# A two-layer decoder trunk in fp32: inverse sums earlier, masks chained by head, the output weights fetched and split on another schedule

## The chip, the cores and the metric

The kernel runs on one core of one Trainium2 chip. The metric is the device time of one execution in microseconds (us). Five engines work side by side, each with its own list of instructions in a fixed order: TensorE (PE in the profile, with its weight loads as PEld), VectorE (DVE), ScalarE (ACT), GpSimd (POOL) and SyncE (SP). All DMAs of this stretch are issued by SP, one after the other in SP's order. An instruction starts when it is first in its engine's order and the semaphores it waits for have been raised.

## The reference, cut to what matters

Two layers work on x (1024 x 1024, fp32). Layer 0 mixes with causal pooling. Layer 1, where the change lies, mixes with a forgetting attention of 16 heads of 64 channels:

```python
logits = einsum('bqhd,bkhd->bhqk', q, k) * scale        # blocks of 128 queries
logits = logits + (cum_q[..., :, None] - cum_k[:, :, None, :])
logits = where(kpos <= qpos, logits, -inf)
p = softmax(logits)
out = einsum('bhqk,bkhd->bqhd', p, v)
...
h = x @ w_in                      # main | mem q | main gate | mem gate
y = concat([y_main * silu(g_main), y_mem * silu(g_mem)])   # 1024 + 512 channels
x = layer_norm(ALPHA * x + y @ w_out)                      # in each layer
```

Each layer also has a cross-attention of 4 heads to 256 memory tokens (y_mem).

## The kernel before, in words

**Tiling.** The sequence is 8 tiles of 128 rows, the channels 8 blocks of 128. A product in fp32 is made from three products of parts: every operand is split into a high part and the rest (`hi_lo`, L138: a copy on ACT at L140, a subtraction on DVE at L141). For weights that come in while the attention runs (`low[0]` set, L850) the split is on POOL (`gp_hi_lo`, L143: L144 and L145).

**Order.** PE's order is written out by hand: the attention and its fill run under a manual schedule of PE (L846 to L852). On ACT, DVE, POOL and SP a scheduler places the instructions, by their traced order and its own estimates, and adds the waits. So a line that stands earlier in the source need not stand earlier on its engine. The words of the changed kernel that pin or chain instructions bind this scheduler.

**Buffers.** Tiles are taken from pools by tag. Of the tag `raw` there are 4 buffers (L113). They hold the unsplit 128 x 512 pieces of all weights: those of a slab (`split_w`, L147 to L152, two pieces to a slab), those of W_out (`OutProj.fetch`, L345 to L351) and two pieces of y1d that `early` reads (L386). A new `raw` takes the buffer that was taken longest ago, and its DMA waits until that buffer's last reader is done. The split weights of slabs lie in the tag `w`, 6 buffers.

**A slab** (L169) is 48 matmuls of 512 columns: two weight pieces, two halves of the sequence, four blocks, three products. It yields after each, so that other code on PE can be put between them. `gate_units` (L259) is a slab whose two results go through `gate` (L190): tanh on ACT (L192), then one DVE instruction (L193).

**The attention** (`fox`, L781) goes over heads `hd` 0 to 16 and within a head over its eight tiles, from tile 7 (longest row of keys) down to tile 0; at `hd` 16 it only drains. One step of it is:

- `probs` (L692): one POOL instruction masks the diagonal block of the head's row tile R (L702). PE makes the logits in one or two parts (`mm3`, L167, into the two PSUM buffers of tag L). A DVE instruction for each part adds R and takes the running extreme (L709). Then comes `behind()`, which is `halves` of the step before (its inverse sum at L726 or L728 with the reciprocal of L729, then ACT L732 and DVE L733 for each part), and then the exponentials on ACT with their sums (L715).
- `fill.pump` (L52): so many matmuls of the waiting slabs.
- `turn` (L738): SP transposes the step-before probabilities by a DMA.
- `values` (L744): matmuls of probabilities and values for a pair of tiles, five steps behind, closed by ACT L758 and DVE L759. After an odd head `pair_out` (L764) multiplies with the gate on POOL and SP writes to y1d (L770).

R of the next head is asked for at the third step of a head (DMA from cumd).

**The last pair.** Heads 14 and 15 (`pr == 7`, L819) have 16 steps, `step` 0 to 15. Their fill is the slab of gate 7 (steps 0 to 3) and the late gates of pairs 3, 5 and 6 (`late_gate`, L772), one slab to four steps. A late gate reads its rows of y1d into an R buffer, multiplies on POOL (L778) and writes them back (L779). Beside this, W_out begins to come in: 24 pieces in all, of which `OutProj.fetch` issues the first ones and `split` splits them through `hi_lo`, and `early` (L382) reads and splits two pieces of y1d and later makes the first output products. In the kernel before, these calls stand ahead of `probs` in a step:

```python
if step == 7: lead = out_proj.early(...)
if step in (7, 9, 10, 12): next(lead)
out_proj.split(min(step - 1, 6) if step < 14 else step - 7)
out_proj.fetch(min(step + 1, 6) if step < 12 else min(step - 5, 8))
```

So piece 0 is fetched at step 0 and split at step 2, piece 5 is split at step 7, pieces 6 and 7 at steps 14 and 15. After the attention, `rest` (L394) splits the other 16 pieces and makes all the other output products (L376), and `norm` (L416) ends the layer.

Of the kernel before, what the change touches and what calls it, by code (L numbers as in the profile page):

```python
# [2 lines left out]

# [6 lines left out]
F32 = mybir.dt.float32  # L10
# [5 lines left out]
ALU = mybir.AluOpType  # L16
AX = mybir.AxisListType

P = 128
# [12 lines left out]
NEG = -1.0e30  # L32
# [39 lines left out]
def trunk_kernel(ctx, tc, x, xT, memT, win, wk, wv0, wv, wmk, wmv, wout, poolw, pscale, lng, lnb, bforget, out):  # L72
# [5 lines left out]
    nc = tc.nc  # L78
# [15 lines left out]
    def nm(tag):  # L94
        count[0] += 1
        return f"{tag}{count[0]}"

    def sb(shape, tag, bufs, dt=F32, where=None):
        return (where or pool).tile(shape, dt, tag=tag, name=nm(tag), bufs=bufs)

    def ps(shape, tag, bufs):
        return psum.tile(shape, F32, tag=tag, name=nm(tag), bufs=bufs)
# [7 lines left out]
    def MK(shape, dt=F32R):  # L110
        return sb(list(shape), "MK", 4, dt)

    def raw(shape):  # L113
        return sb(list(shape), "raw", 4)
# [4 lines left out]
    def tiny(n, dt=F32):  # L119
        return small.tile([P, n], dt, tag=f"s{n}{dt}", name=nm("s"), bufs=4 if n < 12 else 2)  # L120
# [14 lines left out]

        return tiles

    def hi_lo(hi, lo, src):  # L138

        nc.scalar.copy(hi, src)  # L140
        nc.vector.tensor_tensor(lo, src, hi.bitcast(F32), ALU.subtract)  # L141

    def gp_hi_lo(hi, lo, src):  # L143
        nc.gpsimd.tensor_scalar(hi, src, 1.0, 1.0, ALU.mult, ALU.mult)  # L144
# [19 lines left out]
    def mm3(acc, terms):  # L164

        for i, (a, b) in enumerate(terms):
            nc.tensor.matmul(acc, a, b, start=i == 0, stop=i == len(terms) - 1)  # L167
# [168 lines left out]
    class OutProj:  # L336
# [13 lines left out]
                nc.sync.dma_start(r, wout[self.l, n // 2 % 2, 2 * self.KKS[n // 4] + n % 2])  # L350
                self.raws.append(r)  # L351

        def split(self, upto):

            while self.n < upto:
                self.fetch(self.n + 1)
                n = self.n
                kk, nh, j = self.KKS[n // 4], n // 2 % 2, n % 2
                if j == 0:
                    self.ws[nh][kk] = self.wtile(n // 2)  # L360
                h, lo = self.ws[nh][kk]
                hi_lo(h[j], lo[j], self.raws.pop(0))
                self.n += 1

        def open(self, banks=(("pj", 3),) * 2 + (("L", 2),) * 2):
# [16 lines left out]
        def early(self, yh, yl):  # L382


            for j in range(2):
                r, two = raw([P, 2, 2 * P]), slice(2 * j, 2 * j + 2)  # L386
                nc.sync.dma_start(r, self.yd[2, :, two, : 2 * P])
                yield
                hi_lo(yh[:, two, :], yl[:, two, :], r)
                yield  # L390
            self.accs = self.open()
            yield from self.products(self.accs, 2, yh, yl)
# [79 lines left out]
    with tc.tile_pool(name="in0", bufs=1) as in0:  # L472
# [50 lines left out]
        out_proj = OutProj(0, w_slots(wtags, in0), y0d)  # L523
# [12 lines left out]
    with tc.tile_pool(name="in1", bufs=1) as in1:  # L536
# [135 lines left out]
        def start_units(own, following):  # L672
# [11 lines left out]
            next(gates)  # L684
            yield from islice(following, 30)

        def forget_rows(hd):
            R = sb([P, S], "R", 2, F32, in1)
            nc.sync.dma_start(R, cumd[hd].partition_broadcast(P))
            return R  # L690

        def probs(hd, i, R, sums, behind):  # L692

            q, kx, ky = pairs[hd // 2][hd % 2]
            L = (i + 1) * P
            qs = slice(i * P, L)  # L700
            p = MK([P, S], F32)
            nc.gpsimd.affine_select(R[:, qs], R[:, qs], [[-1, P]], ALU.is_ge, -NEG, base=0, channel_multiplier=1)  # L702
            m = tiny(2)
            top = -NEG
            parts = [(0, L)] if L <= NH else [(0, 384), (384, L)] if L == 640 else [(0, NH), (NH, L)]
            for n, (lo, up) in enumerate(parts):
                lg = ps([P, NH], "L", 2)[:, : up - lo]
                mm3(lg, ((q[:, qs], kx[:, lo:up]), (q[:, qs], ky[:, lo:up])))
                nc.vector.tensor_tensor_reduce(p[:, lo:up], lg, R[:, lo:up], 1.0, top, ALU.add, ALU.min, m[:, n : n + 1])  # L709
                top = m[:, n : n + 1]  # L710
            behind()
            es = []
            for n, (lo, up) in enumerate(parts):
                e = ps([P, NH], "T", 2)[:, : up - lo]
                nc.scalar.activation(  # L715
                    e, p[:, lo:up], AF.Exp, bias=top, scale=-1.0, accum_out=sums[:, n, hd % 2, i : i + 1],
                )
                es.append((lo, up, e))
            return hd, i, es, sums

        def halves(hd, i, es, sums):

            L, r = (i + 1) * P, tiny(1)
            one, two = (sums[:, n, hd % 2, i : i + 1] for n in range(2))
            if len(es) == 2:
                nc.vector.tensor_scalar(r, one, two, 1.0 / PSCALE, ALU.add, ALU.mult)  # L726
            else:
                nc.vector.tensor_scalar(r, one, 1.0 / PSCALE, None, ALU.mult)  # L728
            nc.vector.reciprocal(r, r)  # L729
            pair = sb([P, 2 * S], "P", 4, F16)  # L730
            for lo, up, e in es:
                nc.scalar.activation(pair[:, lo:up], e, AF.Copy, scale=r)  # L732
                nc.vector.scalar_tensor_tensor(pair[:, L + lo : L + up], e, r, pair[:, lo:up], ALU.mult, ALU.subtract)  # L733
            return hd, i, pair
# [46 lines left out]
        def fox(following, out_proj):  # L781
            fill, past, fresh = Fill(), [None] * LAG, [None]
            gs = {}

            def gate_ahead(pr):
                gs[pr] = G()
                fill.add(gate_units(win[1, 12 + pr], gs[pr], XH, XL), SLAB)

            ahead_R = forget_rows(0)
            for hd in range(HEADS + 1):  # L790
                pr, b = divmod(hd, 2)
                if hd == HEADS:
                    fill.add(lead, SLAB)
                if hd < HEADS:
                    if b == 0:
                        o, sums = G(), sb([P, 4 * ST], "sums", 2, F32, small).rearrange("p (n b i) -> p n b i", n=2, b=2)
                        if 0 < pr < 7:
                            fill.add(pair_units(pr + 1), 3 * SLAB)
                        for ahead in {0: (0, 1), 2: (2,), 4: (4,), 7: (7,)}.get(pr, ()):
                            gate_ahead(ahead)  # L800
                            if ahead == 0:
                                fill.add(following, SLAB)
                        for late in (3, 5, 6) if pr == 7 else ():
                            fill.add(late_gate(late), SLAB)
                    R, ahead_R = ahead_R, None
                for i in range(ST if hd < HEADS else LAG):
                    tile_of = ST - 1 - i
                    ahead = sum(SHARE[i:]) + (sum(SHARE) if b == 0 else 0)
                    part = fill.left * SHARE[i] / (ahead if hd < HEADS else sum(SHARE[i:LAG]))
                    new, split = None, []  # L810

                    def behind():
                        if fresh[0]:
                            split.append(halves(*fresh[0]))
                            fresh[0] = None

                    if i == 2 and hd < HEADS - 1:
                        ahead_R = forget_rows(hd + 1)
                    if pr == 7:  # L819
                        step = b * ST + i  # L820
                        if step == 7:
                            lead = out_proj.early(*(xy((P, 4, 2 * P)) for _ in range(2)))
                        if step in (7, 9, 10, 12):
                            next(lead)
                        out_proj.split(min(step - 1, 6) if step < 14 else step - 7)
                        out_proj.fetch(min(step + 1, 6) if step < 12 else min(step - 5, 8))
                    if hd < HEADS:
                        new = (hd, tile_of, o)
                        fresh[0] = probs(hd, tile_of, R, sums, behind)
                    else:  # L830
                        behind()
                    fill.pump(part * FRAC[0])
                    for what in split:
                        turn(*what)
                    older = past[0]
                    if older and older[1] % 2 == 0:
                        values(older[0], older[1] // 2, older[2])
                        if older[0] % 2:
                            pair_out(older[0] // 2, older[1] // 2, older[2], gs.get(older[0] // 2))
                    fill.pump(part * (1 - FRAC[0]))  # L840
                    past = past[1:] + [new]
                if b or hd == HEADS:
                    fill.pump(float("inf"))

        wtags = [("MK", 4), ("V", 4)] + [("B", 10)] * 4 + [("w", 0), ("MK", 4), ("R", 2), ("V", 4), ("PG", 0), ("B", 10)]
        out_proj = OutProj(1, w_slots(wtags, in1), y1d)  # L846
# [68 lines left out]
```

## Time and profile before

| What | us |
|---|---|
| Three runs | 1277.45, 1277.76, 1273.79; median 1277.45 |
| The profiled execution | 1275.16 |
| Its span | 1273.4 |
| PE busy within the span | 1243.5 |
| DVE busy | 803.8 |
| ACT busy | 578.5 |
| POOL busy | 174.2 |

The profile is of one execution, and its times are counted from the start of its span. The attention runs from about 672 to 1127 us, its last pair of heads from about 1057 us. A row of the timeline has start, duration, engine, line, operation, names of output and inputs, shape and a count of like instructions; in brackets stands how long the engine was idle before it and what released it. Starts and durations of matmuls overlap, since they are pipelined. L167 writing to L is a logits matmul, L167 writing to O a matmul of values, L179 a matmul of a slab. In the rows a stage by stage view gives (windows), the busy time and count of PE, PEld, DVE, ACT and POOL stand in this order, then the granted PE clock (1.00 is full) and the share and rate of the DMAs.

### The profile page before, as it was taken

The page shows a single profiled execution, that of the slowest core. Times are in us where ns is not written, and L with a number is a line of the kernel's source. Part 1 is how long each engine was busy: PE and PEld are TensorE (multiplying, and loading weights), DVE is VectorE, ACT ScalarE, POOL GpSimd, SP SyncE. Part 2 cuts the span into 40 slices and gives each one's busy share as a digit, 9 for nine tenths or more (in the row PEclk, how much of TensorE's full clock was granted, in tenths as well). Part 3 has the DMA queues.
Part 4 walks back from the last instruction along what each step waited for, and adds up shares of the span by engine and source line. Part 5 has one row for each costly group of instructions (what it writes and reads, how often), then busy time and mean ns, then how long its engine had stood idle before and what let it go on. Part 6 is the DMA issues. An engine that isn't in the chain of part 4 may idle for free. (4 is left out here: it accounts for less than half of the span.)

```text
span 1273.4 us, 19681 instructions
## 1 busy us (share of the span) xinstructions
PE 1243.5 (98%) x7018; PEld 1032.7 (81%) x7018; DVE 803.8 (63%) x1901; ACT 578.5 (45%) x1273; POOL 174.2 (14%) x276
## 2 busy tenths in 40 slices
PE   9999999999999999999999999999999999899997
PEld 6888888888888888888887778887887777777885
DVE  6444766376455555377456878777877887664644
ACT  5233643242321123266225777666667677652110
POOL 0000000000000000000013334342333323430000
PEclk9999999999999999999999999999999999999999
DMA  6333444232553324244516786867877687884430
GB/s 224 108 100 100 117 117 132 83 119 89 158 197 100 106 84 134 75 116 115 162 51 180 137 184 155 195 157 175 187 160 178 157 196 171 209 224 149 166 115 34
DMA packets 267427, 178.66 MB, mean 140 GB/s; under 512 B 212288, under 2 KB 225728, under 8 KB 267328
## 3 DMA queue, kind: packets, MB, share of 16 engines
q1 hardware_dynamic: 267328, 177.40, 52.3%
q8 instruction: 55, 0.90, 0.3%
q14 instruction: 44, 0.36, 0.1%
HBM read 94.97 MB, written 22.61 MB: 92 GB/s over the span
## 5 line engine op out<-in xcount | busy, mean ns | idle before, releaser
L179 PE MATMUL pj<-A,w 128*128 128x512 f32 x2928 | 723.4, 395 | 0.8 <-ACT A L140 0.8
L179 PEld LDWEIGHTS pj<-A,w 128*128 128x128 f32 x2928 | 536.5, 188 | 103.9 <-ACT A L140 2.4
L141 DVE TENSOR_TENSOR w<-raw,w 128x512 fp32r<-128x512 f32 x106 | 74.0, 700 | 105.9 <-ACT w L140 105.1
L715 ACT ACTIVATE T<-MK,s 128x512 f32<-128x512 f32 x192 | 110.8, 577 | 53.1 <-DVE s L709 39.6
L140 ACT CAST w<-raw 128x512 fp32r<-128x512 f32 x106 | 65.7, 621 | 149.8 <-PE pj L179 103.0
L733 DVE SCALAR_TENSOR_TENSOR P<-T,s,P 128x512 f16<-128x512 f32 x192 | 111.5, 613 | 29.8 <-ACT P L732 27.6
L732 ACT ACTIVATE P<-T,s 128x512 f16<-128x512 f32 x192 | 102.7, 576 | 45.5 <-issue 17.2
L167 PE MATMUL L<-B,B 128*128 128x512 f32 (+3 forms) x384 | 92.0, 344 | 14.5 <-DVE s L709 14.1
L167 PEld LDWEIGHTS L<-B,B 128*128 128x128 f32 x384 | 69.8, 188 | 36.8 <-DVE s L709 23.9
L619 POOL MEMSET G<- 128x128 f32 x1 | 0.2, 205 | 610.2 <-DVE V L333 610.2
L709 DVE CUSTOM_DVE_ANT_0 MK<-L,R 128x512 f32<-128x512 f32 (+3 forms) x128 | 72.9, 570 | 12.0 <-PE L L167 7.2
L167 PEld LDWEIGHTS <-V 128*128 128x128 f16 x1152 | 65.2, 99 | 18.6 <-issue 18.6
L167 PE MATMUL O<-T,V 128*128 128x128 f16 x1152 | 76.2, 221 | 1.1 <-DVE G L759 1.1
L141 DVE TENSOR_TENSOR T<-T,T 128x1024 fp32r<-128x1024 f32 x23 | 28.1, 1223 | 70.2 <-PE L L376 51.3
L145 POOL TENSOR_TENSOR w<-raw,w 128x512 fp32r<-128x512 f32 x54 | 70.6, 1307 | 3.8
L140 ACT CAST T<-T 128x1024 fp32r<-128x1024 f32 x23 | 24.2, 1050 | 98.4 <-DMA T<-y0d 50.6
L702 POOL TENSOR_SCALAR_AFFINE_SELECT R<-R 128x128 f32<-128x128 f32 x128 | 42.7, 336 | 180.4 <-DVE s L709 99.2
L144 POOL TENSOR_SCALAR w<-raw 128x512 fp32r<-128x512 f32 x54 | 35.8, 664 | 139.9 <-PE pj L179 131.3
L212 PE MATMUL pj<-T,w 128*128 128x256 f32 x384 | 48.7, 284 | 0.9 <-DVE w L141 0.8
L212 PEld LDWEIGHTS pj<-T,w 128*128 128x128 f32 x384 | 47.6, 192 | 2.0 <-DVE w L141 1.3
L376 PE MATMUL pj<-B,T 128*128 128x512 f32 x186 | 46.5, 392 | 0.5 <-DVE T L141 0.5
L376 PE MATMUL L<-B,T 128*128 128x512 f32 x174 | 43.0, 391 | 0.0
(214 smaller groups left out, 1598.1 us busy)
## 6 DMA issues: line engine op xcount, KB each, us to landing
raw<-in_win_dram SPq DMA_DIRECT2D x96, 256.0 KB, 2.8
raw<-in_wout_dram SPq DMA_DIRECT2D x48, 256.0 KB, 2.9
B<-B SPq DMA_DIRECT2D x32, 256.0 KB, 4.0
R<-cumd SPq DMA_DIRECT2D x16, 512.0 KB, 4.3
y0d<-Y SPq DMA_DIRECT2D x12, 512.0 KB, 3.1
T<-y0d SPq DMA_DIRECT2D x12, 512.0 KB, 3.9
T<-y1d SPq DMA_DIRECT2D x11, 512.0 KB, 4.3
raw<-in_wmk_dram SPq DMA_DIRECT2D x16, 256.0 KB, 2.6
```

The source lines that it names most:

```text
L140: nc.scalar.copy(hi, src)
L141: nc.vector.tensor_tensor(lo, src, hi.bitcast(F32), ALU.subtract)
L145: nc.gpsimd.tensor_tensor(lo, src, hi.bitcast(F32), ALU.subtract)
L167: nc.tensor.matmul(acc, a, b, start=i == 0, stop=i == len(terms) - 1)
L179: nc.tensor.matmul(accs[n], a[:, k, :], b[:, kt, n * NH : (n + 1) * NH], start=kt == 0 and i == 0, stop=kt == KT - 1 and i == 2,)
L212: nc.tensor.matmul(acc, w[:, k, :], m[pc][:, k, :], start=pc == 0 and k == 0 and i == 0, stop=pc == 1 and k == 3 and i == 2,)
L376: nc.tensor.matmul(accs[a][nh], y[:, k, a * P : (a + 1) * P], w, start=kt == 8 and i == 0, stop=kt == 7 and i == 2,)
L702: nc.gpsimd.affine_select(R[:, qs], R[:, qs], [[-1, P]], ALU.is_ge, -NEG, base=0, channel_multiplier=1)
L709: nc.vector.tensor_tensor_reduce(p[:, lo:up], lg, R[:, lo:up], 1.0, top, ALU.add, ALU.min, m[:, n : n + 1])
L715: nc.scalar.activation(e, p[:, lo:up], AF.Exp, bias=top, scale=-1.0, accum_out=sums[:, n, hd % 2, i : i + 1],)
L732: nc.scalar.activation(pair[:, lo:up], e, AF.Copy, scale=r)
L733: nc.vector.scalar_tensor_tensor(pair[:, L + lo : L + up], e, r, pair[:, lo:up], ALU.mult, ALU.subtract)
```

## The change

It has four parts. (1) `inverse_of` is taken out of `halves` and is called inside `probs` of the next tile, behind the first part's DVE instruction. (2) Each mask on POOL is bound to come behind the mask traced before it, so that the masks stand in order of heads and steps. (3) In the last pair the fetches of W_out follow a new list by step, ahead of `probs`; the splits follow another list, behind `probs`, and are pinned: an instruction handed to `keep_in_program_order` stays behind all that was traced before it on its engine. The pieces are split one to a step from step 3 to step 8 (before: steps 2 to 7), the last two at steps 13 and 14. `early` begins at step 9, with its two reads at steps 9 and 12 ahead of `probs` and its two splits at steps 11 and 15 behind it (before: 7, 9, 10, 12). (4) The two splits of `early` are pinned as well. No arithmetic, shape or count of instructions changes.

```diff
--- before.py
+++ after.py
@@ -1,4 +1,4 @@
-from contextlib import ExitStack
+from contextlib import ExitStack, nullcontext
 from itertools import islice
 
 import concourse.bass as bass
@@ -135,10 +135,11 @@
 
         return tiles
 
-    def hi_lo(hi, lo, src):
-
-        nc.scalar.copy(hi, src)
-        nc.vector.tensor_tensor(lo, src, hi.bitcast(F32), ALU.subtract)
+    def hi_lo(hi, lo, src, pinned=False):
+
+        pin = tc.keep_in_program_order if pinned else lambda ins: ins
+        pin(nc.scalar.copy(hi, src))
+        pin(nc.vector.tensor_tensor(lo, src, hi.bitcast(F32), ALU.subtract))
 
     def gp_hi_lo(hi, lo, src):
         nc.gpsimd.tensor_scalar(hi, src, 1.0, 1.0, ALU.mult, ALU.mult)
@@ -350,7 +351,7 @@
                 nc.sync.dma_start(r, wout[self.l, n // 2 % 2, 2 * self.KKS[n // 4] + n % 2])
                 self.raws.append(r)
 
-        def split(self, upto):
+        def split(self, upto, pinned=False):
 
             while self.n < upto:
                 self.fetch(self.n + 1)
@@ -359,7 +360,7 @@
                 if j == 0:
                     self.ws[nh][kk] = self.wtile(n // 2)
                 h, lo = self.ws[nh][kk]
-                hi_lo(h[j], lo[j], self.raws.pop(0))
+                hi_lo(h[j], lo[j], self.raws.pop(0), pinned)
                 self.n += 1
 
         def open(self, banks=(("pj", 3),) * 2 + (("L", 2),) * 2):
@@ -386,7 +387,7 @@
                 r, two = raw([P, 2, 2 * P]), slice(2 * j, 2 * j + 2)
                 nc.sync.dma_start(r, self.yd[2, :, two, : 2 * P])
                 yield
-                hi_lo(yh[:, two, :], yl[:, two, :], r)
+                hi_lo(yh[:, two, :], yl[:, two, :], r, True)
                 yield
             self.accs = self.open()
             yield from self.products(self.accs, 2, yh, yl)
@@ -684,12 +685,14 @@
             next(gates)
             yield from islice(following, 30)
 
+        masked = []
+
         def forget_rows(hd):
             R = sb([P, S], "R", 2, F32, in1)
             nc.sync.dma_start(R, cumd[hd].partition_broadcast(P))
             return R
 
-        def probs(hd, i, R, sums, behind):
+        def probs(hd, i, R, sums, inverse, behind):
 
 
 
@@ -699,7 +702,10 @@
             L = (i + 1) * P
             qs = slice(i * P, L)
             p = MK([P, S], F32)
-            nc.gpsimd.affine_select(R[:, qs], R[:, qs], [[-1, P]], ALU.is_ge, -NEG, base=0, channel_multiplier=1)
+            with tc.issue_after(masked[-1]) if masked else nullcontext():
+                masked.append(
+                    nc.gpsimd.affine_select(R[:, qs], R[:, qs], [[-1, P]], ALU.is_ge, -NEG, base=0, channel_multiplier=1).ins
+                )
             m = tiny(2)
             top = -NEG
             parts = [(0, L)] if L <= NH else [(0, 384), (384, L)] if L == 640 else [(0, NH), (NH, L)]
@@ -708,6 +714,8 @@
                 mm3(lg, ((q[:, qs], kx[:, lo:up]), (q[:, qs], ky[:, lo:up])))
                 nc.vector.tensor_tensor_reduce(p[:, lo:up], lg, R[:, lo:up], 1.0, top, ALU.add, ALU.min, m[:, n : n + 1])
                 top = m[:, n : n + 1]
+                if n == 0:
+                    inverse()
             behind()
             es = []
             for n, (lo, up) in enumerate(parts):
@@ -718,15 +726,19 @@
                 es.append((lo, up, e))
             return hd, i, es, sums
 
-        def halves(hd, i, es, sums):
-
-            L, r = (i + 1) * P, tiny(1)
+        def inverse_of(hd, i, n, sums):
+            r = tiny(1)
             one, two = (sums[:, n, hd % 2, i : i + 1] for n in range(2))
-            if len(es) == 2:
+            if n == 2:
                 nc.vector.tensor_scalar(r, one, two, 1.0 / PSCALE, ALU.add, ALU.mult)
             else:
                 nc.vector.tensor_scalar(r, one, 1.0 / PSCALE, None, ALU.mult)
             nc.vector.reciprocal(r, r)
+            return r
+
+        def halves(hd, i, es, r):
+
+            L = (i + 1) * P
             pair = sb([P, 2 * S], "P", 4, F16)
             for lo, up, e in es:
                 nc.scalar.activation(pair[:, lo:up], e, AF.Copy, scale=r)
@@ -809,6 +821,11 @@
                     part = fill.left * SHARE[i] / (ahead if hd < HEADS else sum(SHARE[i:LAG]))
                     new, split = None, []
 
+                    def inverse():
+                        if fresh[0]:
+                            old, k, es, of = fresh[0]
+                            fresh[0] = old, k, es, inverse_of(old, k, len(es), of)
+
                     def behind():
                         if fresh[0]:
                             split.append(halves(*fresh[0]))
@@ -818,17 +835,21 @@
                         ahead_R = forget_rows(hd + 1)
                     if pr == 7:
                         step = b * ST + i
-                        if step == 7:
+                        out_proj.fetch((0, 1, 2, 3, 4, 5, 6, 6, 6, 6, 7, 7, 8, 8, 8, 8)[step])
+                        if step == 9:
                             lead = out_proj.early(*(xy((P, 4, 2 * P)) for _ in range(2)))
-                        if step in (7, 9, 10, 12):
+                        if step in (9, 12):
                             next(lead)
-                        out_proj.split(min(step - 1, 6) if step < 14 else step - 7)
-                        out_proj.fetch(min(step + 1, 6) if step < 12 else min(step - 5, 8))
                     if hd < HEADS:
                         new = (hd, tile_of, o)
-                        fresh[0] = probs(hd, tile_of, R, sums, behind)
+                        fresh[0] = probs(hd, tile_of, R, sums, inverse, behind)
                     else:
+                        inverse()
                         behind()
+                    if pr == 7:
+                        out_proj.split((0, 0, 0, 1, 2, 3, 4, 5, 6, 6, 6, 6, 6, 7, 8, 8)[step], True)
+                        if step in (11, 15):
+                            next(lead)
                     fill.pump(part * FRAC[0])
                     for what in split:
                         turn(*what)
```

## The prediction, made before the changed kernel had run

> **What bounds the kernel now.** The first part of the page gives the busy time of each engine; the view of waits, kept to PE, gives what PE waited for.
>
> ```profile
> PE 1243.5 (98%) x7018; PEld 1032.7 (81%) x7018; DVE 803.8 (63%) x1901; ACT 578.5 (45%) x1273; POOL 174.2 (14%) x276
> ```
>
> ```profile
> PE L L167 <- DVE s L709: 14.1, 15, 3.1
> ```
>
> PE is busy for 1243.5 of 1273.4 us, and its list of instructions is the same in both kernels, row for row. So time can come only from PE's pauses and its clock. Nearly half of the pauses are one kind: 15 waits of the logits matmuls (L167) for a DVE extreme (L709) that has yet to empty their buffer, 14.1 us in all. The change is about these. I then looked for the 15 in PE's timeline; the largest lie in the last pair.
>
> ```profile
> 1070.74 2.91 PE L179 MATMUL pj<-A,w 128*128 128x512 f32 x12
> 1076.03 0.73 PE L167 MATMUL L<-B,B 128*128 128x512 f32 x2 [2.39 <-DVE s L709]
> 1076.60 1.32 PE L179 MATMUL pj<-A,w 128*128 128x512 f32 x5
> ...
> 1102.82 0.73 PE L167 MATMUL L<-B,B 128*128 128x512 f32 x2 [3.11 <-DVE s L709]
> 1104.01 0.50 PE L167 MATMUL L<-B,B 128*128 128x256 f32 x2 [0.46 <-DVE s L709]
> ```
>
> What held DVE stands in the timelines of ACT and DVE:
>
> ```profile
> 1070.48 0.62 ACT L140 CAST B<-raw 128x512 fp32r<-128x512 f32 x1 [1.90 <-DMA raw<-in_wout_dram]
> ...
> 1098.41 1.32 ACT L140 CAST B<-raw 128x512 fp32r<-128x512 f32 x2 [3.87 <-DMA raw<-in_wout_dram]
> ```
>
> ```profile
> 1071.63 0.49 DVE L759 SCALAR_TENSOR_TENSOR G<-O,unscale,G 64x256 f32<-64x256 f32 x1 [1.17 <-ACT G L758]
> ...
> 1072.23 0.68 DVE L141 TENSOR_TENSOR V<-raw,V 128x512 fp32r<-128x512 f32 x1
> ...
> 1074.83 0.68 DVE L193 SCALAR_TENSOR_TENSOR G<-G,pj 128x512 f32<-128x512 f32 x1
> 1075.42 0.55 DVE L709 CUSTOM_DVE_ANT_0 MK<-L,R 128x384 f32<-128x384 f32 x1
> ...
> 1101.18 0.21 DVE L726 TENSOR_SCALAR s<-sums 128x1 f32<-128x1 f32 x1 [4.88 <-ACT T L715]
> ...
> 1102.08 0.67 DVE L709 CUSTOM_DVE_ANT_0 MK<-L,R 128x512 f32<-128x512 f32 x1
> ```
>
> Both times a copy of a W_out piece stands on ACT ahead of the work that DVE needs, and ACT waits for that piece's DMA: 1.90 and 3.87 us. DVE then waits behind ACT (for L758 at 1071.63, for the exponentials at 1101.18), and L709 comes late, at 1075.42 and 1102.08. After the second pause the clock falls as well, as three windows of 3.41 us show:
>
> ```profile
> 1098.17:1101.58 3.41, 1.54 (x7) 0.94 (x5) 0.36 (x2) 3.07 (x7) 2.77 (x5) 1.00 0.45 114
> 1101.58:1104.99 3.41, 1.71 (x7) 1.18 (x8) 2.96 (x8) 2.33 (x6) 0.89 (x2) 1.00 0.57 191
> 1104.99:1108.40 3.41, 3.41 (x19) 2.64 (x19) 2.65 (x9) 2.26 (x6) 1.57 (x2) 0.50 0.97 211
> ```
>
> PE was granted 0.50 for one window, so about 1.7 us of work was lost there. After the pause of 2.39 us nothing of this kind follows (PE's five matmuls at 1076.60 take 1.32 us, the rate of the twelve at 1070.74).
>
> **What the change removes.** In the last pair the copies and subtractions of W_out now stand behind the exponentials of their step, and each piece has been on its way two steps or more. The three pauses, 2.39 + 3.11 + 0.46, and the 1.7 of clock go: 7.66 us. What is late next is named below. At worst the clock loss stays, for other reasons: 5.96.
>
> Elsewhere the order of the masks matters:
>
> ```profile
> 759.02 0.54 POOL L702 TENSOR_SCALAR_AFFINE_SELECT R<-R 128x128 f32<-128x128 f32 x2 [6.66 <-DMA R<-cumd]
> ```
>
> ```profile
> 759.60 0.48 DVE L709 CUSTOM_DVE_ANT_0 MK<-L,R,s 128x256 f32<-128x256 f32 x1 [0.80 <-POOL R L702]
> ```
>
> ```profile
> 764.59 0.73 PE L167 MATMUL L<-B,B 128*128 128x512 f32 x2 [1.08 <-DVE s L709]
> ...
> 878.54 0.72 PE L167 MATMUL L<-B,B 128*128 128x512 f32 x2 [1.12 <-DVE s L709]
> ...
> 992.31 0.74 PE L167 MATMUL L<-B,B 128*128 128x512 f32 x2 [0.95 <-DVE s L709]
> ...
> 1045.28 0.73 PE L167 MATMUL L<-B,B 128*128 128x512 f32 x2 [1.21 <-DVE s L709]
> ```
>
> POOL waits 6.66 us for the R of the *next* head while a mask of the current head stands behind it; DVE loses 0.80 us by that and PE stalls five us later. The same pattern stands ahead of the pauses at 878.54 and 992.31. Together they are 3.15 us. In order of heads the masks don't wait so, but DVE is also crowded there by other work, so I take two thirds, 2.2 (0 to 3.15). The moved inverse is two one-column instructions; they sit in front of or behind an L709 of the same step. In the built order nothing else of DVE or ACT moves up to about 1028 us, so there I count the move at nothing: it is hidden by DVE's idle time. Ahead of the pause at 1045.28 one DVE instruction of 0.7 us (L657) goes from in front of the L709 to behind it: 0.7 of the 1.21 (0 to 1.21). Gains outside the last pair: 2.9 us (0 to 4.36).
>
> **What the change adds.** W_out pieces and slab weights share four `raw` buffers. A later split holds a buffer longer, and in the built order of the changed kernel the DMA of late gate 3's first weight piece waits for the DVE subtraction of W_out piece 0. That subtraction is pinned at step 3. The scheduler has put on DVE, in front of it, the closing instruction of gate 7 (L193), and on ACT, in front of its copy, the tanh of gate 7 and the two exponentials of step 3. So it can't run until gate 7's *last* matmul is done. But after that matmul PE has only the two logits matmuls of the next tile, and then late gate 3's first matmul, which needs the piece. The wait is a chain from the end of one slab to the start of the next. Its links, from the groups by shape between 640 and 1130 us, and from two issues with their POOL split:
>
> ```profile
> L192 ACT ACTIVATE G<-pj 128x512 f32<-128x512 f32 x16 | 9.5, 592 | 6.7 <-PE pj L179 5.4 <-PE L L167 1.3
> ...
> L715 ACT ACTIVATE T<-MK,s 128x384 f32<-128x384 f32 x48 | 27.5, 574 | 2.7 <-DVE P L733 2.4
> L715 ACT ACTIVATE T<-MK,s 128x256 f32<-128x256 f32 x48 | 22.3, 465 | 4.9 <-DVE s L709 3.6 <-DVE P L733 1.3
> ...
> L140 ACT CAST B<-raw 128x512 fp32r<-128x512 f32 x10 | 6.1, 620 | 7.9 <-DMA raw<-in_wout_dram 5.8 <-DMA raw<-y1d 2.0
> ...
> L144 POOL TENSOR_SCALAR w<-raw 128x512 fp32r<-128x512 f32 x54 | 35.8, 664 | 139.9 <-PE pj L179 131.3 <-DMA raw<-in_win_dram 8.5
> L145 POOL TENSOR_TENSOR w<-raw,w 128x512 fp32r<-128x512 f32 x54 | 70.6, 1307 | 3.8
> ```
>
> ```profile
> 1068.34 0.38 SPq L149 DMA_DIRECT2D raw<-in_win_dram  x1
> ...
> 1074.75 0.33 SPq L149 DMA_DIRECT2D raw<-in_win_dram  x1
> ```
>
> ```profile
> 1071.71 0.63 POOL L144 TENSOR_SCALAR w<-raw 128x512 fp32r<-128x512 f32 x1 [5.77 <-DMA raw<-in_win_dram]
> ...
> 1077.45 0.62 POOL L144 TENSOR_SCALAR w<-raw 128x512 fp32r<-128x512 f32 x1 [2.73 <-DMA raw<-in_win_dram]
> ```
>
> *First wait.* Tanh 0.59, exponentials 0.57 + 0.47, copy 0.62, subtraction 0.68: 2.93 us. From SP's issue to POOL's start 3.37 (1068.34 to 1071.71) or 2.70 (1074.75 to 1077.45). POOL's high part 0.66. Together 6.29 to 6.96 behind gate 7's end; PE is ready 0.57 behind it (1076.03 to 1076.60), so it waits 5.7 to 6.4. The third matmul needs the low part, 1.31 later, of which two matmuls cover 0.5: 0.8 more. 6.5 to 7.2; I take 6.9. In the kernel before, the issue at 1068.34 lies 5 us ahead of gate 7's end, since its buffer came free earlier; hence no such pause there.
>
> *Second wait.* The second piece of late gate 3 waits for the subtraction of W_out piece 2, at step 5, behind the exponential of tile 2. From that tile's logits: L709 0.55, exponential 0.57, copy 0.62, subtraction 0.68, with small steps 2.5; then 2.70 to 3.37 and 0.66: 5.9 to 6.5.
>
> ```profile
> 1080.14 2.92 PE L179 MATMUL pj<-A,w 128*128 128x512 f32 x12
> 1082.91 0.40 PE L167 MATMUL L<-B,B 128*128 128x256 f32 x2
> 1083.14 1.09 PE L179 MATMUL pj<-A,w 128*128 128x512 f32 x4
> ```
>
> PE's work up to the matmul that needs it is the like of these rows, 1080.14 to 1083.14: 3.0. It waits 2.9 to 3.5, with the low part's 0.8 3.7 to 4.3; I take 4.0.
>
> *Third wait.* The first piece of late gate 6 waits for the subtraction of `early`'s first piece (step 11), which again stands behind the end of a slab, late gate 5; on SP it stands also behind a write of y1d that waits for two POOL products.
>
> ```profile
> 1097.89 2.81 POOL L778 TENSOR_TENSOR R<-R,G 128x256 f32<-128x256 f32 x4 [4.92 <-DMA R<-y1d]
> ```
>
> Logits 0.57, L709 0.67 and its read, L193 0.68, two products 1.4: 3.4; issue to POOL 2.70 to 3.37, high part 0.66: 6.8 to 7.4, less 0.57, plus 0.8: 7.0 to 7.7; I take 7.4. For the other pieces (late gate 5's two, late gate 6's second) the same counting gives no pause.
>
> The three are 18.3 us (17.2 to 19.2). Each has a bare pause as long as the 3.11 us that cost a window at 0.50, or longer: 3 x 1.7 = 5.1 us of clock. Bounds: 1.7, if one alone is caught, and 8.5, if each of the two long ones costs two windows.
>
> [...]
>
> Behind the last pair the order of `rest` shifts a little. Its largest pause is this:
>
> ```profile
> 1140.35 0.50 PE L167 MATMUL O<-T,V 128*128 128x128 f16 x6 [1.11 <-DVE G L759]
> ```
>
> It may go or be doubled: 0, with bounds of -1.1 and +1.1.
>
> **The sum,** against the profiled execution's own 1275.16 us (2.3 below the median of the runs): - 7.66 - 2.9 + 18.3 + 5.1 = **1288 us**. Low end: 1275.16 - 7.66 - 4.36 + 17.2 + 1.7 - 1.1 = 1280.9. High end: 1275.16 - 5.96 + 19.2 + 8.5 + 1.1 = 1298.
>
> **The rivals.** *The shared buffers don't hold PE* (ends on the other side). If the pieces of the late gates land ahead of the slab's end, as the one issued at 1068.34 did, only the gains are left: 1275.16 - 7.66 - 2.9 = 1264.6. It decides by whether the subtraction of W_out piece 0 runs some 6 us ahead of gate 7's end. For it: ACT and DVE are busy for only 45% and 63% of the span. Against it: the built order puts the tanh of gate 7's end in front, and an engine doesn't pass over what stands first.
> *Only one of the three waits reaches PE,* because after the first pause the other engines are ahead: 1264.6 + 6.9 + 1.7 = 1273 to 1275.
> *Longer landings.* One W_out issue took from 1093.94 to ACT's 1098.41:
>
> ```profile
> 1093.94 0.86 SPq L350 DMA_DIRECT2D raw<-in_wout_dram  x2
> ```
>
> That is 4.47 us, 1.4 more than my middle value of 3.04; three times this, and the clock's upper bound, give 1288 + 4.2 + 3.4 = 1295.6.
> *No clock loss:* 1288 - 5.1 = 1283.
> *Masks and inverse do nothing outside the last pair,* since the pauses come from a crowded DVE and not from the mask: 1288 + 2.9 = 1291.
>
> **Chances.** Forecast as summed 0.45, longer landings 0.15, masks without effect 0.12, no clock loss 0.10, one wait alone 0.06, no wait 0.07, worse than all of this 0.05. The range 1280 to 1299 holds the first four, 0.82. What a measurement of this kernel can tell from no change is about 0.3%, 3.8 us, so 1273.6 to 1281.3 counts as the same: faster 0.07, same 0.06, slower 0.87.
>
> **What would show it.** In the changed kernel's profile PE should show three pauses released by POOL (w, L144 or L145) in front of L179: of some 6, 3 and 6 to 7 us, at the starts of late gate 3, its second piece and late gate 6, each with a pause of about 0.8 behind it, and windows at 0.50 behind them. The pauses named L709 in the last pair should be gone, ACT's waits for raw<-in_wout_dram too, and the pauses near 764, 878 and 992 smaller. POOL's waits for R<-cumd should shrink from the 6.66 us shown. I am wrong if POOL's L144 doesn't wait for raw<-in_win_dram behind the slabs' ends.

## The result, and the profile after

| | us | runs |
|---|---|---|
| Before, median | 1276.39 (1273.79 to 1277.76) | 5 |
| Changed, median | 1289.53 (1287.31 to 1290.61) | 5 |
| Ratio | 1.0102, 95% interval 1.0087 to 1.0117 | |
| Span of the profiled execution, before and changed | 1273.4 and 1288.6 | |

The changed kernel is slower by 13.1 us in the medians and by 15.2 us in the profiled spans. The forecast was 1288. In the changed source the lines stand a little lower: L709 is L715 now, L144 and L145 are L145 and L146, L167 is L168, L179 is L180, L702 is L707, L759 is L771. These are PE's line of the page, and PE's waits of 2 us and more:

```profile
PE 1248.5 (97%) x7018; PEld 1036.2 (80%) x7018; DVE 803.2 (62%) x1901; ACT 578.9 (45%) x1273; POOL 172.0 (13%) x276
```

```profile
PE pj L180 <- POOL w L145: 18.7, 3, 8.1
PE L L168 <- DVE s L715: 4.5, 10, 0.9
PE O L168 <- DVE G L771: 2.3, 1, 2.3
```

A wait that was not there, on POOL's split of slab weights, came three times and holds 18.7 us. The wait that the change is about fell from 14.1 to 4.5. PE is busy for 5.0 us longer with the same matmuls, which the windows further down put down to the clock. And a wait for values (L771) grew from 1.1 to 2.3. Together: + 18.7 - 9.6 + 5.0 + 1.2 = + 15.3, against 15.2 of span. Nothing else of size is left to explain.

The three pauses in PE's timeline, with the logits ahead of the first:

```profile
1069.41 0.61 PE L168 MATMUL L<-B,B 128*128 128x512 f32 x2
1077.45 3.01 PE L180 MATMUL pj<-A,w 128*128 128x512 f32 x5 [7.42 <-POOL w L145]
...
1090.59 3.00 PE L180 MATMUL pj<-A,w 128*128 128x512 f32 x5 [3.19 <-POOL w L145]
...
1124.89 3.01 PE L180 MATMUL pj<-A,w 128*128 128x512 f32 x5 [8.10 <-POOL w L145]
```

The chain ahead of the first pause can be read link by link in the timelines of ACT, DVE, SP and POOL; the later rows belong to the second and third pauses:

```profile
1069.76 1.05 ACT L744 ACTIVATE P<-T,s 128x512 f16<-128x512 f32 x2 [0.98 <-ACT G L193]
1070.70 0.60 ACT L193 ACTIVATE G<-pj 128x512 f32<-128x512 f32 x1
...
1072.37 0.60 ACT L141 CAST MK<-raw 128x512 fp32r<-128x512 f32 x1
```

```profile
1073.00 0.69 DVE L142 TENSOR_TENSOR MK<-raw,MK 128x512 fp32r<-128x512 f32 x1
...
1086.50 0.69 DVE L142 TENSOR_TENSOR V<-raw,V 128x512 fp32r<-128x512 f32 x1 [0.16 <-ACT V L141]
...
1118.60 1.00 DVE L142 TENSOR_TENSOR B<-raw,B 128x512 fp32r<-128x512 f32 x1
```

```profile
1073.72 0.33 SPq L150 DMA_DIRECT2D raw<-in_win_dram  x1
...
1087.22 0.33 SPq L150 DMA_DIRECT2D raw<-in_win_dram  x1
...
1120.21 0.32 SPq L791 DMA_DIRECT2D y1d<-R  x1
1120.58 0.42 SPq L150 DMA_DIRECT2D raw<-in_win_dram  x1
```

```profile
1076.63 0.76 POOL L145 TENSOR_SCALAR w<-raw 128x512 fp32r<-128x512 f32 x1 [1.97 <-DMA raw<-in_win_dram]
...
1089.92 0.62 POOL L145 TENSOR_SCALAR w<-raw 128x512 fp32r<-128x512 f32 x1 [1.25 <-DMA raw<-in_win_dram]
...
1118.33 1.85 POOL L790 TENSOR_TENSOR R<-R,G 128x256 f32<-128x256 f32 x2 [0.32 <-DVE G L194]
1124.22 0.62 POOL L145 TENSOR_SCALAR w<-raw 128x512 fp32r<-128x512 f32 x1 [4.04 <-DMA raw<-in_win_dram]
```

Tanh of gate 7's end at 1070.70, copy of the W_out piece at 1072.37, its subtraction to 1073.69, SP's issue of the weights at 1073.72, POOL at 1076.63, PE at 1077.45. The longest link is the transfer with 2.91 us, and the engines' own are under 0.8 each; it is a row of hand-overs across five queues, and PE stands at its end. The second pause has the same links: the subtraction ends at 1087.19, SP issues at 1087.22, POOL starts at 1089.92. At the third pause the last to come is the other branch. The subtraction was done at 1119.60, but two products on POOL lasted to 1120.18, the write of y1d stands behind them on SP, and only then come the weights at 1120.58. So about 1.0 us of this pause is the order on SP and not the buffer.

Windows behind the first, second and third pause (the granted clock is the number in front of the last two):

```profile
1077.87:1081.28 3.41, 3.27 (x12) 1.93 (x12) 0.00 (x0) 0.12 (x1) 0.88 (x1) 0.50 0.58 154
1081.28:1084.69 3.41, 3.41 (x11) 2.73 (x11) 0.62 (x2) 0.35 (x1) 0.00 (x0) 0.64 0.75 231
...
1091.51:1094.92 3.41, 3.28 (x27) 2.37 (x27) 0.00 (x0) 0.00 (x0) 2.26 (x3) 0.64 0.37 125
...
1125.61:1129.02 3.41, 3.27 (x13) 2.06 (x12) 0.00 (x0) 0.41 (x1) 0.67 (x2) 0.50 0.46 154
1129.02:1132.43 3.41, 3.41 (x12) 2.75 (x11) 0.75 (x2) 0.06 (x1) 1.81 (x2) 0.63 0.59 90
```

Busy time times what the clock lacks: 3.27 x 0.50 + 3.41 x 0.36 = 2.9 behind the first, 1.2 behind the second, 2.9 behind the third: 7.0 us of PE's work lost, where the kernel before lost 1.7.

The pauses answered for by the masks, at the places of 764.59, 878.54 and 992.31 before:

```profile
762.89 0.73 PE L168 MATMUL L<-B,B 128*128 128x512 f32 x2 [0.44 <-DVE s L715]
...
876.18 0.73 PE L168 MATMUL L<-B,B 128*128 128x512 f32 x2 [0.44 <-DVE s L715]
...
989.48 0.72 PE L168 MATMUL L<-B,B 128*128 128x512 f32 x2 [0.44 <-DVE s L715]
```

They fell from 1.08, 1.12 and 0.95 to 0.44 each. In the last pair no copy on ACT waits for a DMA any more. The change did all that it says; a resource that it doesn't name took more than it gave.

### The profile page after: what moved, and what is told of

Read it like the earlier page. It is cut to its first block, busy times and chain, and to the rows that moved or that the text cites. A ratio compares the mean times of both kernels' runs of the same rounds, so it can differ in the third digit from the quotient of the medians.

```text
span 1288.6 us, 19680 instructions
## 1 busy us (share of the span) xinstructions
PE 1248.5 (97%) x7018; PEld 1036.2 (80%) x7018; DVE 803.2 (62%) x1901; ACT 578.9 (45%) x1273; POOL 172.0 (13%) x276
## 5 line engine op out<-in xcount | busy, mean ns | idle before, releaser
L180 PE MATMUL pj<-A,w 128*128 128x512 f32 x2928 | 729.8, 397 | 20.3 <-POOL w L145 18.7
L180 PEld LDWEIGHTS pj<-A,w 128*128 128x128 f32 x2928 | 539.1, 189 | 126.5 <-POOL w L145 19.7
L744 ACT ACTIVATE P<-T,s 128x512 f16<-128x512 f32 x192 | 102.8, 576 | 44.3 <-ACT T L723 17.5
L168 PE MATMUL L<-B,B 128*128 128x512 f32 (+3 forms) x384 | 91.1, 343 | 5.2 <-DVE s L715 4.5
L168 PEld LDWEIGHTS L<-B,B 128*128 128x128 f32 x384 | 70.5, 188 | 26.2 <-DVE s L715 12.7
L715 DVE CUSTOM_DVE_ANT_0 MK<-L,R 128x512 f32<-128x512 f32 (+3 forms) x128 | 72.9, 570 | 16.1 <-PE L L168 12.8
L168 PEld LDWEIGHTS <-V 128*128 128x128 f16 x1152 | 65.4, 99 | 20.3 <-issue 20.0
L168 PE MATMUL O<-T,V 128*128 128x128 f16 x1152 | 76.4, 221 | 2.3 <-DVE G L771 2.3
L146 POOL TENSOR_TENSOR w<-raw,w 128x512 fp32r<-128x512 f32 x54 | 69.7, 1290 | 3.8
L707 POOL TENSOR_SCALAR_AFFINE_SELECT R<-R 128x128 f32<-128x128 f32 x128 | 41.1, 327 | 192.2 <-DVE s L715 164.3
L145 POOL TENSOR_SCALAR w<-raw 128x512 fp32r<-128x512 f32 x54 | 35.4, 656 | 137.1 <-PE pj L180 126.0
```

What stands on the lines that cost most here:

```text
L146: nc.gpsimd.tensor_tensor(lo, src, hi.bitcast(F32), ALU.subtract)
L180: nc.tensor.matmul(accs[n], a[:, k, :], b[:, kt, n * NH : (n + 1) * NH], start=kt == 0 and i == 0, stop=kt == KT - 1 and i == 2,)
```

## The experiments

The theory: W_out pieces and slab weights share the ring of four `raw` buffers, and later, pinned subtractions hand a buffer back only behind a slab's end. The rivals are that the splits slow PE whatever buffer they use, and that POOL or the DMA is late by itself. Each run is compared with the kernel before on the same chip, which took 1275.2 to 1275.3 us in the median.

**e1: two rings of two buffers.** While the attention runs, slab weights take one ring, W_out and `early` the other; together they hold as much as the ring of four. Two steps of the lists move as well.

```diff
-    def raw(shape):
-        return sb(list(shape), "raw", 4)
+    turns = [0]
+
+    def raw(shape, of_out=False):
+        turns[0] += 1
+        return sb(list(shape), ("raw", "rawo")[of_out if low[0] else turns[0] % 2], 2)
...
-                r = raw([P, NH])
+                r = raw([P, NH], True)
...
-                r, two = raw([P, 2, 2 * P]), slice(2 * j, 2 * j + 2)
+                r, two = raw([P, 2, 2 * P], True), slice(2 * j, 2 * j + 2)
...
-                        out_proj.fetch((0, 1, 2, 3, 4, 5, 6, 6, 6, 6, 7, 7, 8, 8, 8, 8)[step])
+                        out_proj.fetch((0, 1, 2, 2, 3, 4, 5, 6, 6, 6, 7, 7, 7, 8, 8, 8)[step])
...
-                        out_proj.split((0, 0, 0, 1, 2, 3, 4, 5, 6, 6, 6, 6, 6, 7, 8, 8)[step], True)
+                        out_proj.split((0, 0, 0, 1, 2, 3, 4, 5, 6, 6, 6, 6, 7, 7, 7, 8)[step], True)
```

> The changed kernel, with the four raw buffers as two rings of two while the attention runs: one for the weights of slabs, one for the pieces of W_out and of y1d (fetch and split lists moved by a step where two buffers ask for it). Theory (the W_out subtractions hold the shared buffers and so the slab weights): the three pauses of PE for POOL L145's like, 18.7 us, go and the half clock behind them with them, so only the gains are left: 1264 to 1268 us. Rival (the later splits slow PE through busy DVE and ACT or through DMA traffic, whatever buffer they use): 1283 to 1291, with pauses of the same size named otherwise.

Measured: 1262.18 us (1259.73 to 1264.23), ratio 0.9887 (0.9862 to 0.9911). PE has no wait for POOL left, and its matmuls keep one rate all through the last pair: each twelve of a slab take 2.90 to 2.95 us, as the 2.91 in the kernel before. The time is 1.8 us below the range of the theory, so the mechanism holds and only its size was missed; the rival, that later splits slow PE whatever their buffer, falls.

**e10: the same two rings, with the changed kernel's own lists,** so the first three hunks above and nothing else.

> The changed kernel with two rings of two and nothing else: fetch and split lists exactly as changed. Theory (sharing alone made the three pauses, not the moved steps of the first two-ring run): no PE wait for POOL, 1261 to 1266. Rival (the moved lists did it): the three pauses or like ones, 1280 or more.

Measured: 1260.69 us (1259.42 to 1262.26), ratio 0.9880 (0.9851 to 0.9908). This is just below the range of the theory. Sharing made the pauses; the moved lists of e1 have no part in it. This is faster than both kernels. Its lines stand three lower than in the changed source. Its views are PE's line of the page, PE's waits, and the first piece of late gate 3 on SP, on POOL and on PE:

```profile
PE 1241.4 (98%) x7018; PEld 1033.2 (82%) x7018; DVE 802.6 (64%) x1901; ACT 578.1 (46%) x1273; POOL 172.5 (14%) x276
```

```profile
PE L L171 <- DVE s L718: 6.2, 13, 1.3
PE pj L183 <- ACT A L144: 1.3, 1, 1.3
```

```profile
1043.97 0.33 SPq L153 DMA_DIRECT2D raw<-in_win_dram  x1
```

```profile
1055.51 0.63 POOL L148 TENSOR_SCALAR w<-raw 128x512 fp32r<-128x512 f32 x1 [4.45 <-PE pj L183]
```

```profile
1072.12 1.29 PE L183 MATMUL pj<-A,w 128*128 128x512 f32 x5
```

The weights are asked for at 1043.97, 28 us ahead of PE's use of them at 1072.12, and POOL's split at 1055.51 waits for PE, not for a DMA. PE is busy for 7.1 us less than in the changed kernel, with the same matmuls. That agrees with the 7.0 us of clock from the windows only roughly, since at another place, at 678 us, nine matmuls take 1.5 us longer in e10 (3.76 us against 2.24, shown at the end).

**e4: one number moved,** the split of W_out piece 0, to step 2.

```diff
-                        out_proj.split((0, 0, 0, 1, 2, 3, 4, 5, 6, 6, 6, 6, 6, 7, 8, 8)[step], True)
+                        out_proj.split((0, 0, 1, 1, 2, 3, 4, 5, 6, 6, 6, 6, 6, 7, 8, 8)[step], True)
```

> The changed kernel with one number different: piece 0 of W_out is split at step 2 in place of step 3, so that its subtraction stands ahead of the end of gate 7. Theory: the first of the three pauses (7.4 us) goes with its 3 us of half clock, the other two stay (3.2 and 8.1): 1278 to 1281. Rival (the pauses are the DMA's or POOL's own delay): all three stay, 1289.

Measured: 1289.12 us (1287.88 to 1289.95), ratio 1.0095 (1.0071 to 1.0120). My expectation was wrong. PE's timeline shows where the gain went:

```profile
1070.74 0.73 PE L168 MATMUL L<-B,B 128*128 128x512 f32 x2 [1.21 <-DVE s L715]
1073.30 0.80 PE L180 MATMUL pj<-A,w 128*128 128x512 f32 x2 [1.82 <-POOL w L145]
1074.66 1.65 PE L180 MATMUL pj<-A,w 128*128 128x512 f32 x3 [0.56 <-POOL w L146]
...
1088.92 3.00 PE L180 MATMUL pj<-A,w 128*128 128x512 f32 x5 [5.20 <-POOL w L145]
...
1124.29 3.00 PE L180 MATMUL pj<-A,w 128*128 128x512 f32 x5 [8.22 <-POOL w L145]
```

The first chain starts earlier, but a step is only some 3.5 us and the chain over 6, so 1.82 + 0.56 of it still shows, with 1.21 of a logits wait in front. The second pause grew from 3.19 to 5.20: PE came to it 3.7 us earlier (its logits at 1083.33, before at 1087.01), but its weights were asked for only 2.5 us earlier (1084.70, before 1087.22) and took 3.55 us to POOL in place of 2.70. In all, PE's idle time fell by 2.1 us and its busy time grew by 1.7 (1250.2 against 1248.5; behind the first pause 0.50 was granted from 1073.90 to 1077.30 and 0.51 to 1080.70), so half clock took nearly all of it back. In this kernel a chain that was cut by less than its length passed the rest on.

**e3: the new schedule and pins alone,** without the mask chain, and with the inverse back in its place:

```diff
-            with tc.issue_after(masked[-1]) if masked else nullcontext():
-                masked.append(
-                    nc.gpsimd.affine_select(R[:, qs], R[:, qs], [[-1, P]], ALU.is_ge, -NEG, base=0, channel_multiplier=1).ins
-                )
+            nc.gpsimd.affine_select(R[:, qs], R[:, qs], [[-1, P]], ALU.is_ge, -NEG, base=0, channel_multiplier=1)
...
-                if n == 0:
-                    inverse()
...
+                        inverse()
                         if fresh[0]:
                             split.append(halves(*fresh[0]))
```

> The changed kernel without the mask chain and with the inverse where it was: the new schedule of W_out and the pins alone. Theory: the three pauses stand as in the changed kernel, 18 to 19 us with 4 to 5 us of clock, and the small pauses at 764, 878, 992 are back: 1291 to 1294. Rival (the pauses need the new order of masks on POOL, in front of the weight split): 1264 to 1276.

Measured: 1295.12 us (1294.4 to 1298.6), ratio 1.0151 (1.0127 to 1.0175). PE's waits on POOL:

```profile
PE pj L180 <- POOL w L145: 17.8, 3, 7.4
```

The three pauses stand without the new order of masks, so they belong to the third and fourth parts of the change, the new schedule with its pins. The time is 1.1 us above the range I gave. The waits for DVE are longer again (L710 there): 8.8 us in all against 4.5. The first two parts are worth some 5 to 6 us to the changed kernel (spans of 1294.0 and 1288.6, ratios of 1.0151 and 1.0102), and 2.9 us of that stand in PE's busy time.

**e8: the changed kernel without pins.**

```diff
-                        out_proj.split((0, 0, 0, 1, 2, 3, 4, 5, 6, 6, 6, 6, 6, 7, 8, 8)[step], True)
+                        out_proj.split((0, 0, 0, 1, 2, 3, 4, 5, 6, 6, 6, 6, 6, 7, 8, 8)[step])
...
-                hi_lo(yh[:, two, :], yl[:, two, :], r, True)
+                hi_lo(yh[:, two, :], yl[:, two, :], r)
```

> The changed kernel without the pins: the scheduler may place the splits of W_out and of early where it likes. Theory (the pinned place behind the slab's end makes the chain): some of the three pauses shrink, 1270 to 1285. Rival (the steps alone decide, the pins change nothing): 1288 to 1290.

Measured: 1267.81 us (1266.67 to 1268.55), ratio 0.9933 (0.9916 to 0.9950), below the range I gave. No wait of PE for POOL is left. So it takes both: the shared ring, and the pin that holds the subtraction behind the slab's end. The scheduler moves the splits ahead by itself: the first two subtractions of W_out start at 1061.31, where the changed kernel has them at 1073.00 and 1076.22. PE's longest wait is one of the old kind, 2.56 us:

```profile
1061.31 1.37 DVE L142 TENSOR_TENSOR V<-raw,V 128x512 fp32r<-128x512 f32 x2
```

```profile
1091.91 0.74 PE L168 MATMUL L<-B,B 128*128 128x512 f32 x2 [2.56 <-DVE s L715]
```

**e9: e1 without pins,** by the same two lines.

> The two rings with their moved lists, without the pins. Theory (with rings apart, the pins do what they say: they keep W_out's copies behind the exponentials, and cost nothing): the scheduler again puts some copy ahead, a pause of 1 to 3 us for L718 in the last pair, 1263 to 1267. Rival (a pin is a loss in itself): faster than the pinned 1262.

Measured: 1266.86 us (1265.91 to 1270.73), ratio 0.9935 (0.9913 to 0.9957). With rings apart the pins are worth some 5 to 6 us (1266.86 against e1's 1262.18, and by the ratios 0.9935 and 0.9887). PE's longest pause in the last pair is 1.97 us here, and none is over 0.5 in e1 and e10. Copies on ACT that wait for their DMA stand ahead of other work again, as before the change (in e10 copies wait too, the longest near the same place 1.38 us at 1083.75, but without such a pause):

```profile
1087.23 0.62 ACT L144 CAST B<-rawo 128x512 fp32r<-128x512 f32 x1 [1.86 <-DMA rawo<-y1d]
```

**e7: masks, inverse and two rings, with W_out on the schedule of before, unpinned.**

```diff
+                        if step == 7:
+                            lead = out_proj.early(*(xy((P, 4, 2 * P)) for _ in range(2)))
+                        if step in (7, 9, 10, 12):
+                            next(lead)
+                        out_proj.split(min(step - 1, 6) if step < 14 else step - 7)
+                        out_proj.fetch(min(step + 1, 6) if step < 12 else min(step - 5, 8))
```

(in place of the changed kernel's lines in `fox`, on top of e10; `early` is not pinned either.)

> Masks and inverse as changed, two rings of two raw buffers, but W_out fetched and split on the schedule of before, unpinned. Theory (what the new schedule is worth by itself are the two pauses of 2.39 and 3.11 us, with 0.46 and 1.7 of clock, which a copy that waits on ACT makes): those pauses stay, 1270 to 1273. Rival (separate buffers alone remove them, since the pieces come earlier): 1262 to 1265, as with the two rings and the new schedule.

Measured: 1268.70 us (1268.24 to 1270.11), ratio 0.9943 (0.9926 to 0.9959). It fell between the two ranges, so neither was right. One pause of the old kind is left, 2.12 us; the next in size in the last pair is 0.88. So the new schedule with its pins is worth some 8 us (1268.70 against 1260.69) where it has its own buffers.

**e2, e5, e6: the first two parts.** e2 is the changed kernel with W_out on the schedule of before (e7's lines, one ring); e5 is before with the mask chain alone; e6 is e2 without the mask chain:

```diff
+            with tc.issue_after(masked[-1]) if masked else nullcontext():
+                masked.append(
+                    nc.gpsimd.affine_select(R[:, qs], R[:, qs], [[-1, P]], ALU.is_ge, -NEG, base=0, channel_multiplier=1).ins
+                )
...
+                if n == 0:
+                    inverse()
```

(the first hunk in e5 and e2, the second in e6 and e2.)

> The kernel before with masks in order of heads and the inverse moved, and W_out as before. Theory: pauses near 764, 878 and 992 shrink by about two thirds, the two pauses of 2.39 and 3.11 in the last pair stay: 1272 to 1275 where before has 1276. Rival (crowded DVE makes those pauses, not the mask): no difference, 1276.

> The kernel before with the masks in order of heads and nothing else. Theory (the mask that waits for the next head's R makes the pauses near 764, 878 and 992): each falls from about 1 us to about 0.45, some 1.8 us in all: 1273 to 1274 where before has 1275. Rival (the moved inverse did it): no difference.

> The kernel before with the inverse moved and nothing else. Theory: the order of DVE and ACT is unchanged up to 1028 us, so the pauses at 764, 878, 992 stay at about 1 us; the one at 1045 (1.21 us) may go: 1274 to 1275.5. Rival (the inverse carries the gain of the pair): 1272.

Measured: e2 1272.10 us, ratio 0.9969 (0.9957 to 0.9982); e5 1273.00 us, ratio 0.9983 (0.9971 to 0.9995); e6 1274.37 us, ratio 0.9984 (0.9971 to 0.9996). PE's timelines at the four places, first of e5, then of e6:

```profile
762.25 0.73 PE L167 MATMUL L<-B,B 128*128 128x512 f32 x2 [0.46 <-DVE s L714]
...
875.56 0.72 PE L167 MATMUL L<-B,B 128*128 128x512 f32 x2 [0.46 <-DVE s L714]
...
988.85 0.73 PE L167 MATMUL L<-B,B 128*128 128x512 f32 x2 [0.46 <-DVE s L714]
...
1041.85 0.73 PE L167 MATMUL L<-B,B 128*128 128x512 f32 x2 [1.18 <-DVE s L714]
```

```profile
764.73 0.73 PE L168 MATMUL L<-B,B 128*128 128x512 f32 x2 [1.87 <-DVE s L710]
...
879.64 0.74 PE L168 MATMUL L<-B,B 128*128 128x512 f32 x2 [0.57 <-DVE s L710]
...
994.54 0.74 PE L168 MATMUL L<-B,B 128*128 128x512 f32 x2 [1.87 <-DVE s L710]
```

The masks alone bring the three pauses to 0.46 and leave the one at 1041.85. The inverse alone leaves the three uneven, up to 1.87, and takes the fourth away: no row of e6 stands at its place. POOL's wait for R<-cumd went with the masks too. Its row before, then in e5 (us in total, times, longest):

```profile
POOL R L702 <- DMA R<-cumd: 45.2, 11, 8.8
```

```profile
POOL R L706 <- DMA R<-cumd: 0.4, 1, 0.4
```

So both halves of the early gain are settled, though each is at the edge of what a time can tell.

## Why the prediction was right

**The new wait, right.** The three pauses came at the three places named, released by POOL's split; e1 and e10 show that the shared ring makes them, and e8 that the pins do their part. That the sizes agree so well, 18.7 us against 18.3, is partly luck. The 18.3 hold 0.8 for each pause that never came, 2.4 us; without it the forecast was 15.9, and the pauses themselves were 2.8 longer. The first was 7.42 against 6.1 and 0.8: from the tanh to the subtraction's end I counted 2.93 and the trace has 2.99, but tanh itself started 1.3 us after the logits did, behind two instructions of the step before (L744), which I had left out. What I had added for the low part, 0.8 to each pause, does not show as a pause of its own. That fits the clock: at the granted 0.50 five of these matmuls took 3.01 us, so the two ahead of it some 1.2 (an estimate), nearly the 1.28 of POOL's low part; and in e4, where the first two took only 0.80 us, 0.56 of it shows. The second was 3.19 against 3.2 and 0.8. The third was 8.10 against 6.6 and 0.8: the weights took 3.64 us from SP (1120.58) to POOL (1124.22), where I had 2.70 to 3.37, and the two products 1.85 where I had 1.4. Behind this pause I had named both branches, and the write of y1d was the later one.

**What the change removes, right.** 5.96 + 2.9 = 8.9 us of pauses forecast, 9.6 found. The mask's share was forecast as 2.2 and is 1.8 (1.08 + 1.12 + 0.95 less 3 x 0.44). The pause of 1.21 at 1045.28 went wholly, not by 0.7, and e6 shows that the inverse's move did it.

**The clock, right in kind, too small.** I had 5.1 us for three pauses, at 1.7 each by one row. The two long ones cost 2.9 each, nearly twice that, the short one 1.2: 7.0. The short one, of 3.19 us, cost clock as the 3.11 us of the kernel before had. One part of the account failed: I took the length of a pause as what decides, and in other runs matmuls were slow behind shorter ones too (see the last section).

**Behind the last pair,** I put 0 with bounds of 1.1 to either side; the wait for L771 grew by 1.2.

**The sum:** forecast + 12.8 on the profiled execution's own time; found + 15.2 in the spans and + 13.1 in the medians. Of the 2.4 missing in the spans, and up to rounding, the clock is 1.6 (+ 5.0 found in PE's busy time, + 3.4 forecast), the tail 1.2, the pauses 0.4 more, less 0.7 of larger gains.

**The rival on the other side,** 1264.6 if the buffers don't hold PE, is what e1 and e10 bring about: 1262.18 and 1260.69. It set its point of decision at a subtraction some 6 us ahead of the slab's end; e4, with a step of 3.5 us, fell short of it, and I should have read my own line before I forecast 1278 to 1281 for it.

## What to carry to other kernels

When an operation is moved later, look up what it *holds* while it waits: a buffer ring shared with something on the path turns a harmless delay into a wait for the next user, and the price is the whole chain from release to landing, not the move (here 18.7 us of PE's waits). A pin is a promise about order on one engine; ask what the scheduler has put in front of it (here the end of a slab), and who waits behind. Where two streams share a ring and only one is urgent, split the ring before tuning the order: here that cost no memory and was worth some 28 us (1289.53 to 1260.69).

## What the runs showed of the hardware

In the changed kernel a pause of PE of 3.2 us cost 1.2 us of half clock, and pauses of 7.4 and 8.1 us cost 2.9 each: each was dearer than its length by more than a third. But the length alone doesn't decide. These are the same nine matmuls at the start of the attention, first in the kernel before, then in e10:

```profile
677.04 0.73 PE L167 MATMUL L<-B,B 128*128 128x512 f32 x2 [1.18 <-DVE s L709]
...
678.43 2.24 PE L179 MATMUL pj<-A,w 128*128 128x512 f32 x9
```

```profile
676.65 0.73 PE L171 MATMUL L<-B,B 128*128 128x512 f32 x2 [1.32 <-DVE s L718]
...
678.03 3.76 PE L183 MATMUL pj<-A,w 128*128 128x512 f32 x9
```

Behind a pause of 1.32 us they took 3.76 us, behind one of 1.18 us 2.24, and behind the 2.39 us of the kernel before, in its last pair, no clock was lost (1.00 was granted from 1074.30 to 1081.12). In e6, behind the pause of 1.87 us at 764.73, five matmuls of a slab took 2.34 us at 767.18, where five took 1.40 at 758.05. What decides stays open.

A 256 KB piece of weights took 2.91 us (1073.72 to 1076.63) and 3.64 us (1120.58 to 1124.22) from SP's issue to its first reader, with the same shape and source; what makes the difference stays open.
